# Residual rows and staged operand sums bound to fixed units of the products, and an earlier load of one pair of weights

## The chip, the cores and the metric

The kernel runs on one core of a Trainium2 chip. The time is what the device takes for one launch, in microseconds (us), as the median of several runs. The engines are named as in the profile: PE is TensorE, DVE is VectorE, ACT is ScalarE, POOL is GpSimd, SP is SyncE, which here only issues DMAs.

## The reference

One layer of a hybrid decoder for a prompt of 2048 tokens (with 16 meta tokens ahead of it) and 8 sample tokens; D_MODEL is 1024, D_FF 4096, everything float32.

```python
def _layer(h, s0, buf, chunked, lb, norm1_g, w_in, ..., w_out, norm2_g, w_up, w_down):
    hn = _rmsnorm(h, norm1_g)
    z = jnp.einsum('btd,dc->btc', hn, w_in)
    ...                                    # HGRN2 recurrence || conformer convolution
    h = h + jnp.concatenate([y_hg, y_cv], axis=-1) @ w_out
    hn2 = _rmsnorm(h, norm2_g)
    h = h + jnp.square(jax.nn.relu(hn2 @ w_up)) @ w_down
    return h, s_new, new_buf
...
    y_prompt = _rmsnorm(hp[:, N_META:], final_g)
    y_sample = _rmsnorm(hs, final_g)
```

The change touches the last part, the MLP (`w_up`, squared ReLU, `w_down`, residual, final norm), and the loads ahead of it.

## The kernel before

**Mixer.** About the first 990 us compute the input projection, the recurrence, the convolution and the out-projection, by quarters of the tokens (`q`) and tiles of output columns (`t`). The out-projection leaves h, transposed, in the DRAM tensor `hscr`, and the row of each token's norm factor in `mscr`. Each product is done in fp32r with every operand split in a rounded high half (`hi`) and the rest (`lo`).

**MLP.** The tokens go in three passes `p` (688, 688 and 680 columns; pass 0 holds 680 of the prompt and the 8 of the sample). D_FF goes in 16 groups `g` of 256. A *unit* is twelve matmuls. The up-projection of a group is a Strassen-Winograd scheme of seven products, in the order P1, P5, P6, P3, P7, P2, P4: seven U units, whose epilogues leave the squared ReLU in `hid`. The down-projection of a group is eight D units, whose epilogues add into `acc`. The list `seq` sets the order: in a pass seven U units of group 0; then seven U of group 1 and eight D of group 0; then, from group 2 on, a U unit of group g and a D unit of group g-1 in turn; at the end eight D units of the last group. `steps` holds the position in `seq` of each group's first U unit, over all passes.

**Operands.** `op` and `extra` hold the split token sums that the seven products take, the weight sums of w_up lie in `ups` and `wsp`, and the pieces of w_down come as `junk` or `wsp` (`d_load`, `d_split`). The sums of w_up for the next group, or pair, are made from loads into `raw`, `bst` or `acc` (`up_prep`); their loads and splits are put at units by a dictionary `hooks`, run right after the unit of that number. The operands of pass 0 are made on the fly (`h_first`, `h_rest`). Those of passes 1 and 2 are staged: `h_stage(p + 1)` computes 4 x 7 sums while pass p runs, each as ScalarE high half and VectorE low half in the one buffer `stg`, which SP then stores to `bop_d` in DRAM. In the last group of pass p, as each product gives its operands back, `h_fetch` loads those of the next pass from `bop_d`, 28 transfers in all.

**What sets the order.** Beside the units runs a planner: background tasks (`bg`) are generators which say before each step what engine it is for (`yield "act"`); a model of the engines' times (`model`) puts such steps, by the task's number, where it thinks the engine free. Three such tasks matter here. `residual(p)`, number 6, starts with the first U unit of pass p: it takes both tiles of `xns`, loads the norm row, and for each of 8 row blocks loads a row of `hscr` into the tile `xn`, multiplies it on POOL and adds it into `acc` on VectorE. `h_stage(p + 1)`, number 7, is added after U0 of group 2 and takes the same two tiles. In the last group the program says

```python
if g == NG - 1 and p < NPASS - 1:
    bg.until(lambda: ("staged", p + 1) in done)
    h_fetch(p + 1, PRODUCTS[d][3])
```

which runs the generators until all sums are issued. `fg_load` and `eps_cols` (the row of final_g, and 19 small loads of `emm` out of `mscr`) are added ahead of the first unit of the MLP. The finishing of a pass (`finish`) transposes finished tiles into two free PSUM banks.

**At the entry of the MLP** the weights of the second pair (`up_prep(1)`) go to a tile `raw` and three buffers that are taken from `scr` after the mixer; their four loads are hooks of the first U units.

## Time and profile before

| | us |
|---|---|
| median of 3 runs | 2554.85 |
| the runs | 2554.21, 2554.85, 2560.22 |
| the profiled execution, its own time | 2564.89 |
| its span | 2563.2 |
| PE busy | 2326.5 (91%) |
| DVE busy | 1684.5 (66%) |
| ACT busy | 1055.4 (41%) |
| POOL busy | 666.1 (26%) |

The profile is of one execution; all times that are read from its rows are in us from the start of its span. The mixer ends and the MLP begins at about 987, pass 1 begins at 1555, pass 2 at 2069. Every operation stands at line 146, a helper that records them all, so rows are told apart by their tiles.

### The profile page before, as it was taken

How to read it: one execution, taken by the hardware profiler on the slowest of the kernel's cores; microseconds unless marked ns; L12 is line 12 of the kernel's file. 1: busy time of each engine (PE TensorE's matmuls, PEld its weight loads, DVE VectorE, ACT ScalarE, POOL GpSimd, SP SyncE). 2: the span in 40 equal slices, each digit the busy share in tenths (PEclk: the TensorE clock that was granted, in tenths of full speed). 3: DMA queues.
4: the chain of work that ended last, by engine and by line, in shares of the span. 5: the costliest groups of instructions: out<-in, count | busy, mean ns of one | idle time of the engine just before them, and what ended most of it. 6: DMA issues, size and time to landing. Idle time of an engine off the chain costs nothing.

```text
span 2563.2 us, 37257 instructions
## 1 busy us (share of the span) xinstructions
PE 2326.5 (91%) x13790; PEld 2170.7 (85%) x13790; DVE 1684.5 (66%) x2906; ACT 1055.4 (41%) x2199; POOL 666.1 (26%) x529
## 2 busy tenths in 40 slices
PE   8888899899999996999999848999999689999998
PEld 8877678777877875899999837999999689999997
DVE  7797977488478545467666635577777555765665
ACT  6454544444354333444544424333333333333332
POOL 5552424333254012244333211111010011211000
PEclk9998899999999997999999969999999899999999
DMA  8665346834644474355455474445444634443332
GB/s 300 214 203 173 136 176 206 287 132 164 227 169 161 175 257 137 118 159 166 164 188 181 140 249 150 131 129 156 153 153 151 240 122 134 134 121 119 107 107 102
DMA packets 309470, 428.71 MB, mean 167 GB/s; under 512 B 21506, under 2 KB 216391, under 8 KB 292896
## 3 DMA queue, kind: packets, MB, share of 16 engines
q1 hardware_dynamic: 309144, 426.06, 50.8%
q8 instruction: 109, 1.79, 0.3%
q14 instruction: 73, 0.60, 0.1%
q10 hardware_dynamic: 144, 0.26, 0.0%
HBM read 311.75 MB, written 114.97 MB: 166 GB/s over the span
## 4 chain that ended last, share of the span: by engine, by line
PE 46%; DVE 20%; issue 11%; DMA 10%; ACT 5%; POOL 4%; SPq 2%; POOLq 0%; ACTq 0%; DVEq 0%
PE ps L146 46%; DVE ps L146 7%; DMA junk<-in_w_down_dram 4%; SPq L146 2%; DVE stat L146 2%; POOL wsp L146 2%; DMA bst<-in_w_up_dram 2%; DVE acc L146 2%; ACT cst L146 1%; DMA bop_d<-stg 1%; DVE cst L146 1%; POOL ups L146 1%; DVE I L146 1%; DVE kept L146 1%; DVE raw L146 1%
## 5 line engine op out<-in xcount | busy, mean ns | idle before, releaser
L146 PE MATMUL ps<-op,wsp 128*128 128x512 f32 (+6 forms) x5427 | 1063.5, 350 | 23.2 <-DVE op L146 12.4
L146 PEld LDWEIGHTS ps<-op,wsp 128*128 128x128 f32 x5427 | 893.5, 194 | 127.6 <-DVE op L146 14.1
L146 PE MATMUL ps<-hid,wsp 128*128 128x344 f32 (+2 forms) x4512 | 779.9, 324 | 95.3 <-DVE acc L146 61.9
L146 PEld LDWEIGHTS ps<-hid,wsp 128*128 128x128 f32 x4512 | 728.5, 191 | 110.3 <-ACT wsp L146 38.6
L146 DVE TENSOR_TENSOR acc<-ps,acc 128x688 f32<-128x688 f32 (+4 forms) x424 | 346.5, 818 | 319.4 <-PE ps L146 259.6
L146 ACT ACTIVATE cst<-cst 128x344 f32<-128x344 f32 (+1 forms) x384 | 188.4, 491 | 466.6 <-DVE cst L146 460.2
L146 PE MATMUL ps<-op,ups 128*128 128x344 f32 (+1 forms) x2013 | 354.6, 324 | 15.9 <-DVE cst L146 7.2
L146 PEld LDWEIGHTS ps<-op,ups 128*128 128x128 f32 x2013 | 327.7, 192 | 20.0 <-DVE cst L146 6.3
L146 POOL TENSOR_TENSOR acc<-acc 128x512 f32<-128x512 f32 x169 | 225.1, 1332 | 244.4 <-ACT acc L146 227.6
L146 DVE SCALAR_TENSOR_TENSOR ps<-glu,cw,ps 128x512 f32<-128x512 f32 x295 | 221.7, 751 | 5.9
L146 POOL TENSOR_TENSOR wsp<-junk,wsp 128x256 fp32r<-128x256 f32 x128 | 101.7, 796 | 371.2 <-ACT wsp L146 332.0
L146 DVE TENSOR_TENSOR cst<-ps,cst 128x344 f32<-128x344 f32 (+1 forms) x336 | 170.9, 509 | 19.2 <-PE ps L146 15.7
L146 POOL TENSOR_TENSOR ups<-bst,ups 128x512 fp32r<-128x512 f32 x50 | 76.6, 1541 | 297.8 <-ACT ups L146 297.8
L146 DVE TENSOR_TENSOR hid<-cst,hid 128x344 fp32r<-128x344 f32 (+1 forms) x192 | 105.5, 549 | 56.4 <-ACT hid L146 56.1
L146 DVE TENSOR_TENSOR ups<-raw,ups 128x512 fp32r<-128x512 f32 x108 | 79.9, 740 | 89.6 <-ACT ups L146 89.4
L146 POOL TENSOR_TENSOR wsp<-bst,wsp 128x512 fp32r<-128x512 f32 x42 | 63.5, 1521 | 251.3 <-ACT wsp L146 251.3
L146 ACT ACTIVATE acc<-glu,cw 128x512 f32<-128x512 f32 x185 | 123.5, 715 | 1.6 <-DVE glu L146 1.6
L146 DVE TENSOR_TENSOR wsp<-raw,wsp 128x512 fp32r<-128x512 f32 x84 | 64.2, 765 | 57.8 <-ACT wsp L146 57.5
L146 POOL TENSOR_TENSOR wsp<-raw,wsp 128x1024 fp32r<-128x1024 f32 (+1 forms) x34 | 79.1, 2327 | 76.5 <-ACT wsp L146 63.8
L146 ACT ACTIVATE wsp<-junk 128x256 fp32r<-128x256 f32 x128 | 52.2, 409 | 110.5 <-DMA junk<-in_w_down_dram 94.5
L146 ACT ACTIVATE hid<-cst 128x344 fp32r<-128x344 f32 (+1 forms) x192 | 94.2, 491 | 6.1
L146 ACT ACTIVATE wsp<-raw 128x512 fp32r<-128x512 f32 (+1 forms) x118 | 85.9, 728 | 10.8 <-DMA raw<-in_w_in_dram 6.6
(239 smaller groups left out, 2098.0 us busy)
## 6 DMA issues: line engine op xcount, KB each, us to landing
wsp<-kw SPq DMA_DIRECT2D x96, 1024.0 KB, 4.8
wsp<-down_w SPq DMA_DIRECT2D x248, 256.0 KB, 2.7
bst<-in_w_up_dram SPq DMA_DIRECT2D x138, 256.0 KB, 4.7
kw<-wsp SPq DMA_DIRECT2D x32, 1024.0 KB, 5.0
down_w<-wsp SPq DMA_DIRECT2D x128, 256.0 KB, 2.0
bop_d<-stg SPq DMA_DIRECT2D x56, 344.0 KB, 2.7
junk<-in_w_down_dram SPq DMA_DIRECT2D x128, 128.0 KB, 3.4
raw<-in_w_in_dram SPq DMA_DIRECT2D x24, 512.0 KB, 7.7
```

The source lines that it names most:

```text
L146: return fn(*args, **kw)
```

## The change

- **Residual rows and staged sums.** `residual` and `h_stage` are gone. `side_work(p)` returns a list of (unit, function), counted from U0 of group 2 of the pass, which goes into `hooks`. The row block k of the residual is loaded at unit 4k, multiplied at 4k + 2 and added at 4k + 3. From unit 33 on, four blocks of 31 units follow (passes 0 and 1): the two loads, and seven sums at 3, 7, 11, 15, 19, 23 and 28, ScalarE's half at that unit, VectorE's half and the store one unit later. The wait ahead of `h_fetch` has become an assertion.
- **Second pair's weights.** The task `up_first`, which prepares the first pair, takes the three buffers of `scr` as soon as the last input of the out-projection is loaded, and issues the four loads there; the hooks leave them out.
- **fg and emm.** These two tasks are added at the first unit of group 3 of pass 0.
- **Finishing.** `finish` tells the model when its two banks come free.

```diff
@@ -801,6 +801,11 @@
             if n_ == late[0]:
                 scr.give(*got)
+                yield from until(("last out",))
+                up_raws[1] = yield from take(scr, 3)
+                yield "sp"
+                for f in up_prep(1)[0:4]:
+                    f[3]()
                 yield from until(("mix",))
...
                     out_load(q, t)
+                    if q == NQ - 1 and t == K8 - 1:
+                        done.add(("last out",))
...
-        up_raws[1] = [b[:, 0:512] for b in scr.take(3)]
...
-        def residual(p):
...
-            for k in range(K8):
-                yield "sp"
-                h_load(t, p, k)
...
-                yield "pool"
-                G.tensor_tensor(t[:, 0:n], t[:, 0:n], msb[:, 0:n], ALU.mult)
-                yield "dve"
-                V.tensor_tensor(acc[:, k, 0:n], acc[:, k, 0:n], t[:, 0:n], ALU.add)
...
-        def h_stage(p):
...
-            def emit(i, idx, src, scale):
-                yield from split_sum(stg[:, 0, 0:n], stg[:, 1, 0:n], src, scale)
-                yield "sp"
-                SP.dma_start(bop_d[p - 1, i, idx], flat32(stg))
...
+        def side_work(p):
...
+            def rows(k):
+                def times():
...
+                    G.tensor_tensor(t[:, 0:n], t[:, 0:n], tt[:, 0:n], ALU.mult)
+
+                def add():
+                    V.tensor_tensor(acc[:, k, 0:n], acc[:, k, 0:n], t[:, 0:n], ALU.add)
+                    done.add(("res", p, k))
+
+                return [(4 * k, lambda: h_load(t, p, k)), (4 * k + 2, times), (4 * k + 3, add)]
+
             for k in range(K8):
...
+                work += rows(k)
+            at = 4 * K8 + 1
+
+            def staged(i, at):
...
+                def emit(at, idx, src, scale):
+                    def high():
+                        S.activation(hi, src, AF.Copy, scale=1.0 if scale is None else scale)
+
+                    def low():
...
+                        SP.dma_start(bop_d[p, i, idx], flat32(stg))
+
+                    return [(at, high), (at + 1, low)]
+
+                return ([(at, loads)] + emit(at + 3, B11, b11, g) + emit(at + 7, B21, b21, gg) +
+                        emit(at + 11, B22, b22, gg) +
+                        [(at + 14, scaled), (at + 14, lambda: V.tensor_tensor(t1, b12, b11, ALU.subtract))] +
+                        emit(at + 15, T1, t1, g) + [(at + 18, mult_add(t2, t1, ng, t2, ALU.add))] +
+                        emit(at + 19, T2, t2, None) + [(at + 22, mult_add(t1, b21, gg, t2, ALU.subtract))] +
+                        emit(at + 23, T4, t1, None) +
+                        [(at + 26, scaled), (at + 27, mult_add(t2, b12, ng, t2, ALU.add))] +
+                        emit(at + 28, T3, t2, None))
+
+            if p < NPASS - 1:
+                for i in range(4):
+                    work += staged(i, at)
+                    at += 31
...
-            banks.items.remove(b)
-            banks.items.remove(b + 1)
+            for x in (b, b + 1):
+                banks.items.remove(x)
+                model.cur.t = max(model.cur.t, banks.t.get(x, 0.0))
...
-                    if n_ < 4 and G_ % NG == 0 and G_:
+                    if n_ < 4 and G_ == 0:
+                        continue
+                    if n_ < 4 and G_ % NG == 0:
                         at = a - 2
...
-        bg.add(fg_load(), 3)
-        bg.add(eps_cols(), 4)
+        for p in range(NPASS):
+            a = steps[p * NG + 2]
+            for at, f in side_work(p):
+                hooks.setdefault(a + at, []).append(f)
+        hooks[steps[3]].append(lambda: (bg.add(fg_load(), 3), bg.add(eps_cols(), 4)))
...
-                bg.add(residual(p), 6)
...
-                if g == 2 and d == 0 and p < NPASS - 1:
-                    bg.add(h_stage(p + 1), 7)
                 if g == NG - 1 and p < NPASS - 1:
-                    bg.until(lambda: ("staged", p + 1) in done)
+                    assert ("staged", p + 1) in done
                     h_fetch(p + 1, PRODUCTS[d][3])
```

How the order of the instructions changes, at three places. On SP at the entry of the MLP, behind the last store of a norm row (`mscr<-fg`), where `junk` are pieces of w_down, `in_w_up_dram` is the source of the second pair's weights and `down_w<-wsp_87` stores split pieces of w_down; before:

```order
L146 DMA mscr<-fg 1x512
L146 DMA junk<-in_w_down_dram 128x2x128 x2
L146 DMA down_w<-wsp_87 128x512 x2
L146 DMA junk<-in_w_down_dram 128x2x128 x2
L146 DMA fg<-in_final_g_dram 128x1024
L146 DMA emm<-mscr 128x1 x5
```

And after:

```order
L146 DMA mscr<-fg 1x512
L146 DMA raw_85<-in_w_up_dram 128x4x128
L146 DMA acc<-in_w_up_dram 128x4x128 x3
L146 DMA junk<-in_w_down_dram 128x2x128 x2
L146 DMA down_w<-wsp_87 128x512 x2
```

The four loads of the second pair stood behind all of emm and now stand ahead of the first two junk pieces; fg and emm are gone from here, and stand, in the same order, in group 3 of pass 0, behind four loads of weights.

On SP at the end of pass 0, in the last group, where `bop_d<-stg` stores a staged sum, `xn` are the rows from which the sums are made, and `op<-bop_d` is the fetch for pass 1; before:

```order
L146 DMA junk<-in_w_down_dram 128x2x128
L146 DMA bop_d<-stg 128x688 x4
L146 DMA xn_90<-hscr 128x688
L146 DMA xn_91<-hscr 128x688
L146 DMA bop_d<-stg 128x688 x7
L146 DMA op_83<-bop_d 128x2x344 x2
L146 DMA op_84<-bop_d 128x2x344 x2
```

And after:

```order
L146 DMA down_w<-wsp_87 128x512
L146 DMA junk<-in_w_down_dram 128x2x128
L146 DMA op_83<-bop_d 128x2x344 x2
L146 DMA op_84<-bop_d 128x2x344 x2
L146 DMA raw_85<-in_w_up_dram 128x4x128
```

The last eleven stores and the loads for seven of them have left this place; they stand spread between the units of the earlier groups, and the same is so at the end of pass 1.

On DVE at the entry of the MLP, where `raw_85` and `raw_86` take sums of the second pair's weights (in `acc`) and the `op_84` rows are the low halves of pass 0's operands; before:

```order
L146 SCALAR_TENSOR_TENSOR op_84<-acc,vec,op_84 128x344
L146 TENSOR_TENSOR op_84<-bst_7385,op_84 128x344
L146 TENSOR_TENSOR op_84<-bst_7386,op_84 128x344
L146 TENSOR_TENSOR raw_86<-acc,raw_85 128x512
L146 TENSOR_TENSOR raw_85<-raw_85,acc 128x512
L146 TENSOR_TENSOR op_84<-bst_7385,op_84 128x344
L146 TENSOR_TENSOR op_84<-bst_7386,op_84 128x344
```

And after:

```order
L146 TENSOR_TENSOR op_84<-bst_7386,op_84 128x344
L146 TENSOR_TENSOR wsp_88<-raw_85,wsp_88 128x512
L146 SCALAR_TENSOR_TENSOR op_84<-xn_91,vec,op_84 128x344
L146 TENSOR_TENSOR wsp_88<-raw_86,wsp_88 128x512
L146 SCALAR_TENSOR_TENSOR op_84<-acc,vec,op_84 128x344
L146 TENSOR_TENSOR wsp_89<-raw_86,wsp_89 128x512
L146 TENSOR_TENSOR op_84<-bst_7385,op_84 128x344
L146 TENSOR_TENSOR op_84<-bst_7386,op_84 128x344
L146 SCALAR_TENSOR_TENSOR op_84<-xn_91,vec,op_84 128x344
L146 TENSOR_TENSOR raw_86<-acc,raw_85 128x512
L146 TENSOR_TENSOR raw_85<-raw_85,acc 128x512
```

Before, four low halves of this stretch stood ahead of the two sums that need the second pair's loads (`raw_86<-acc,raw_85` and `raw_85<-raw_85,acc`), and the rest of them behind; now the two sums stand behind more of the low halves and behind three splits of first-pair weights.

## Rows read from the trace of the kernel before

**Rows 1.** The page, part 1: engine, busy us (share of the span) x instructions.

```profile
PE 2326.5 (91%) x13790; PEld 2170.7 (85%) x13790; DVE 1684.5 (66%) x2906; ACT 1055.4 (41%) x2199; POOL 666.1 (26%) x529
```

**Rows 2.** The time line of TensorE around the end of pass 0. Columns: start us, duration us, engine, line, operation, output tile <- input tiles, shape, count; in brackets the idle time before it and what ended it. Rows of `op` with `wsp` or `ups` are U units, rows of `hid` are D units.

```profile
1458.29 2.04 PE L146 MATMUL ps<-op,wsp 128*128 128x344 f32 x12
...
1465.85 2.05 PE L146 MATMUL ps<-hid,wsp 128*128 128x344 f32 x12
1467.74 2.07 PE L146 MATMUL ps<-op,ups 128*128 128x344 f32 x12
1501.11 3.78 PE L146 MATMUL ps<-hid,wsp 128*128 128x344 f32 x12 [31.30 <-DVE acc L146]
...
1513.51 3.81 PE L146 MATMUL ps<-op,ups 128*128 128x344 f32 x12 [4.42 <-DVE cst L146]
...
1535.83 5.82 PE L146 MATMUL ps<-hid,wsp 128*128 128x344 f32 x24 [4.59 <-DVE acc L146]
1542.86 12.45 PE L146 MATMUL ps<-hid,wsp 128*128 128x344 f32 x72 [1.21 <-ACT wsp L146]
1555.14 3.46 PE L146 MATMUL ps<-op,wsp 128*128 128x344 f32 x21
```

**Rows 3.** The time line of SP's DMA queue, same place; the last row is the same at the end of pass 1. The duration of a merged row runs from the first issue to the end of the last.

```profile
1463.55 10.44 SPq L146 DMA_DIRECT2D bop_d<-stg  x4
...
1479.49 21.03 SPq L146 DMA_DIRECT2D bop_d<-stg  x7
1500.62 2.59 SPq L146 DMA_DIRECT2D op<-bop_d  x4
...
2015.85 2.51 SPq L146 DMA_DIRECT2D op<-bop_d  x4
```

**Rows 4.** Windows of 4 us, same place: stretch, its length, busy time (x instructions) of PE, PEld, DVE, ACT, POOL, then the granted TensorE clock, the mean share of the DMA engines, GB/s.

```profile
1516.00:1520.00 4.00, 4.00 (x17) 4.00 (x17) 2.88 (x6) 2.29 (x5) 0.50 (x1) 0.58 1.07 388
...
1540.00:1544.00 4.00, 2.79 (x17) 2.31 (x16) 1.40 (x2) 0.83 (x2) 0.87 (x2) 1.00 0.60 211
```

**Rows 5.** The time line of TensorE around the end of pass 1, columns as in rows 2.

```profile
1995.39 2.04 PE L146 MATMUL ps<-op,ups 128*128 128x344 f32 x12
...
2016.25 3.81 PE L146 MATMUL ps<-hid,wsp 128*128 128x344 f32 x12 [10.62 <-DVE acc L146]
...
2027.34 3.78 PE L146 MATMUL ps<-hid,wsp 128*128 128x344 f32 x12 [4.88 <-DVE raw L146]
...
2054.42 15.02 PE L146 MATMUL ps<-hid,wsp 128*128 128x344 f32 x84 [2.08 <-DMA wsp<-down_w]
2069.28 3.89 PE L146 MATMUL ps<-op,ups 128*128 128x340 f32 x24
```

**Rows 6.** The time line of TensorE at the entry of the MLP, columns as in rows 2.

```profile
987.47 2.09 PE L146 MATMUL ps<-op,ups 128*128 128x344 f32 x6
...
995.15 5.24 PE L146 MATMUL ps<-op,ups 128*128 128x344 f32 x17 [2.25 <-DVE op L146]
...
1011.24 1.23 PE L146 MATMUL ps<-op,wsp 128*128 128x344 f32 x3 [9.63 <-DVE op L146]
...
1034.65 3.59 PE L146 MATMUL ps<-op,wsp 128*128 128x344 f32 x12
...
1066.29 2.05 PE L146 MATMUL ps<-op,wsp 128*128 128x344 f32 x12
```

**Rows 7.** The time line of SP's DMA queue at the entry of the MLP.

```profile
988.28 0.24 SPq L146 DMA_DIRECT2D mscr<-fg  x1
988.57 0.90 SPq L146 DMA_DIRECT2D junk<-in_w_down_dram  x2
...
995.10 8.73 SPq L146 DMA_DIRECT2D emm<-mscr  x19
1003.93 0.38 SPq L146 DMA_DIRECT2D raw<-in_w_up_dram  x1
```

**Rows 8.** The time line of VectorE at the entry of the MLP.

```profile
1007.65 0.69 DVE L146 TENSOR_TENSOR raw<-acc,raw 128x512 f32<-128x512 f32 x1 [9.27 <-DMA acc<-in_w_up_dram]
```

**Rows 9.** The time line of ScalarE at the entry of the MLP.

```profile
990.70 0.42 ACT L146 ACTIVATE wsp<-junk 128x256 fp32r<-128x256 f32 x1 [1.85 <-DMA junk<-in_w_down_dram]
...
991.63 0.57 ACT L146 ACTIVATE op<-xn,vec 128x344 fp32r<-128x344 f32 x1
```

**Rows 10.** What is done with the tiles xn between 1060 and 2300 us: engine, operation, output <- input, count, duration in ns (smallest/median/largest), first and last start; below, who waited for these instructions (us, times), and the time from issue to landing of the loads.

```profile
L146 DVE SCALAR_TENSOR_TENSOR stg<-xn,vec,stg x32: 559/566/1175, 1203.6 to 2004.7; 128x344 fp32r<-128x344 f32 x16, 128x340 fp32r<-128x340 f32 x16
L146 POOL TENSOR_TENSOR xn<-xn,xn x24: 1632/1672/2127, 1092.5 to 2247.3; 128x688 f32<-128x688 f32 x16, 128x680 f32<-128x680 f32 x8
...
  DVE acc L146: 5.4, 3
...
DMA to landing us min/median/max: 3.6/4.2/5.8
```

**Rows 11.** The time line of TensorE at the start of pass 1, columns as in rows 2. `ident,acc` are the transposes of finished tiles.

```profile
1562.87 1.22 PE L146 MATMUL ps<-ident,acc 128*128 128x128 f32 x8 [2.05 <-DVE xn L146]
...
1569.17 1.09 PE L146 MATMUL ps<-ident,acc 128*128 128x128 f32 x8 [1.37 <-DVE xn L146]
...
1597.57 1.69 PE L146 MATMUL ps<-ident,acc 128*48 128x128 f32 x8 [2.62 <-DVE xn L146]
```

**Rows 12.** One window of 32 us in the middle of pass 1, columns as in rows 4.

```profile
1856.00:1888.00 32.00, 32.00 (x206) 32.00 (x205) 21.35 (x33) 10.99 (x22) 3.44 (x2) 1.00 0.52 167
```

More of the change, by code (lines that the diff above doesn't have):

```diff
@@ L1610, in eps_cols @@
             done.add(("emm",))
-        def residual(p):
-            yield from until(*[("st", q) for q in quarters(p)], *[("acc", p, k) for k in range(K8)])
-            t, msb = yield from take(xns, 2)
-            yield "sp"
-            SP.dma_start(msb[:, 0:PROMPT[p]],
-                         mscr[:, T0[p]:T0[p] + PROMPT[p]].to_broadcast([P, PROMPT[p]]))
-            if p == 0:
-                SP.dma_start(msb[:, PROMPT[p]:PN[p]], mscr[:, SEQ:SEQ + NS].to_broadcast([P, NS]))
-            n = PN[p]
-            for k in range(K8):
-                yield "sp"
-                h_load(t, p, k)
-                if p == 0:
-                    yield "act"
-                    S.activation(t[:, PROMPT[0]:PN[0]], hsT[:, k], AF.Copy)
-                yield "pool"
-                G.tensor_tensor(t[:, 0:n], t[:, 0:n], msb[:, 0:n], ALU.mult)
-                yield "dve"
-                V.tensor_tensor(acc[:, k, 0:n], acc[:, k, 0:n], t[:, 0:n], ALU.add)
-                done.add(("res", p, k))
-            xns.give(t, msb)
```

61 lines of the change are left out of this document (32 added, 29 removed).

## The prediction

> **What bounds the kernel now.** I read the page first: TensorE is busy 91% of the span [rows 1], so nothing off its path counts unless TensorE waits for it. Then I took the time line of TensorE and looked for the gaps, and for each gap the time line of the engine named in it. A unit of the MLP (twelve matmuls, one U or D) takes 1.89 us when nothing is missing: the units that start at 1465.85 and 1467.74 [rows 2]. Three places are far from that.
>
> *End of pass 0.* From 1458.29 (U0 of the last group) to 1555.14 (first unit of pass 1) are 96.9 us [rows 2] for 7 + 8 + 8 = 23 units, 43.5 us of work: 53.4 us too long. The largest piece is a gap of 31.30 us. In it SP only passes staged sums to DRAM, four and then seven in one row [rows 3]: the generator is run dry there, and each sum needs the one buffer stg, so ScalarE, VectorE and the DMA take turns, about 3 us a sum. VectorE has the accumulations of the units queued behind that chain, which is why the gap is put down to DVE acc. The granted clock stands at 0.58 after it [rows 4] (the 1.2 GHz level for part of the stretch), and two more waits follow, 4.42 and 4.59 us [rows 2]. In the last ones the DMA engines are full: share 1.07 at 388 GB/s, until it drops at 1540 [rows 4].
>
> *End of pass 1.* The same stretch, 1995.39 to 2069.28, is 73.9 us, 30.4 too long; its gaps are 10.62, 4.88 and, at the end of the full DMA, 2.08 us [rows 5].
>
> *Entry of the MLP.* From 987.47 to 1066.29 are 78.8 us for 22 units (41.6 us), 37.2 too long [rows 6]. The longest gap is 9.63 us on a VectorE operand split. VectorE was itself idle 9.27 us for a weight piece of the second pair [rows 8], since SP issued these loads at 1003.93, behind 19 small loads of emm that took 8.73 us [rows 7].
>
> **The change part by part.**
>
> *Staged sums at fixed units.* Nothing is computed that was not before; 56 sums and 24 residual rows move. In pass 0 and pass 1 the order shows no staged store left in front of the first operand fetch, so both gaps of the run-dry chain go. What is late next is the fetch itself: 28 transfers for the next pass, issued as each product releases its operands. They keep the DMA engines full from 1500.62 [rows 3] to about 1541 [rows 4], and TensorE's last wait in the stretch ends at 1542.86 [rows 2]. I therefore don't credit the gap but the shift of the fetch: it now starts when U0 is done, 1458.29 + 2.04 = 1460.3, instead of 1500.6. If the transfers then need as long as before, everything behind them comes 40.3 us earlier, and 13 us of the stretch's excess remain. Pass 1 likewise: the fetch starts after U0 (1995.39 + 2.04 = 1997.4 [rows 5]) in place of 2015.85 [rows 3], so 18 us. Bounds: if TensorE at full clock asks faster and loses to the full queue, the gain is less by the waits that follow the gap, 4.42 + 4.59 in pass 0 and 4.88 + 2.08 in pass 1, giving 31 and 11; if the queue is emptier than before since no staged store overlaps and the weights arrive in time, half of the same waits is gained, giving 44 and 22. I take **-40** and **-18**.
>
> *Second pair's weights and the emm loads.* The order puts the four loads behind the last mscr row, issued at 988.28, so not truly inside the out-projection but about 15 us earlier than 1003.93 [rows 7]. The 9.63 us gap goes. What takes its place: the two junk pieces now stand behind 1 MB of weights. ScalarE has their splits ahead of the operand splits of P1, and got the first at 990.70, about 2 us after issue, the operand split following at 991.63 [rows 9]. One of the four loads waits besides for GpSimd, which reads its buffer. The nearest row for four such loads is 1003.93 to 1007.65, when VectorE gets its first [rows 7, 8]; so junk lands near 995.5, not 990.7. TensorE took up P1 at 995.15 [rows 6] because of VectorE, so of these 5 us about 2 reach it (bounds 0 and 5). Behind the gap, from 1011.24 to 1034.65, TensorE spent 23.4 us on some 53 matmuls, worth 8.3 at 1.89 us for twelve: 15.1 us in small waits and low clock while VectorE caught up [rows 6]. Without the 9 us of standing still it has less to catch up, but the same splits, sums and epilogues stay in its queue; I take half back, 7.5, bounds 0 and 12. Sum -9.6 + 2 - 7.5 = **-15**, bounds -5 and -22.
>
> The pages have a word on the 5 us. The Trainium skill (DMA: Bandwidth & Descriptors, Queues, rings and completion order) says that each DMA engine consumes descriptors of one ring in ring order, which speaks against putting 1 MB ahead of the junk pieces: by it ScalarE stands to about 995.5. Were the pieces served side by side, 993 would do and this part would be worth -17 instead of -15. The row of 990.70, with nothing ahead, doesn't decide between them.
>
> The fg and emm loads now go out in group 3 of pass 0 and hold SP for 8.73 us and a bit there [rows 7]. Queued behind: stores of split down weights and junk loads. A junk piece is asked for four units (7.6 us) ahead of its split and split again four units ahead of its use, so a delay of 8 us holds ScalarE for some 4 us and should just miss TensorE: +1, bounds 0 and 6.
>
> *Residual rows at fixed units.* Each row is load at unit 4k, product on GpSimd at 4k + 2, add on VectorE at 4k + 3; the add stands in VectorE's queue, so if the product is late, every epilogue behind it is too. A load lands in 3.6 to 5.8 us, the product takes 1.67 [rows 10]: 5.3 to 7.5 against the 5.7 us between the points. Before, VectorE waited for products 5.4 us in all [rows 10]. VectorE is busy about 21 of 32 us here [rows 12], and a bank is written again three units after its epilogue fell due, which lets it be behind by some 3 us, so an overrun of 1 us is mostly swallowed. 28 sums now share the groups of pass 0, where 17 did before the eleven of the gap [rows 3]; at 0.57 us for the low half [rows 10] and four more such instructions for seven sums that is some 10 us more VectorE work spread over 245 us. I take +2 for all passes; the bounds are -4 (a few of the small waits at group ends go) and +12 (half a us for each of 24 rows).
>
> *Finishing tiles.* The planner now books a bank's release time, so the transposes move away from the places where TensorE waited 2.05 and 1.37 us for a bank [rows 11]. In exchange the fifth tile now stands directly before the sixth, where 2.62 us were waited already, and both ahead of the first D unit. Gain and loss about cancel: -1, bounds -6 and +5.
>
> *Sum.* -40 - 18 - 15 + 1 + 2 - 1 = -71. The profiled execution took 2564.89 us, so one like it would take 2493.9. It lies 10.0 above the median of the runs, 2554.85; I assume that this distance stays as it is, so the forecast is 2554.85 - 71 = **2484 us**. All good bounds together give -98 (2457), all bad ones -24 (2531); neither is likely as a whole.
>
> **Rivals.**
>
> *The fetch takes it back.* At full clock the products release operands faster than the DMA engines serve, TensorE stalls again inside the group and loses its clock again. For it: share 1.07 already [rows 4]. Against: the fetch was paced by the same units before. With 25 and 5 us gained at the two pass ends the sum is -43: 2512.
>
> *Entry unchanged.* The junk wait on ScalarE and VectorE's own work replace the 9.63 us. For it: 15.1 us of excess that have no single cause [rows 6]. The sum is -56: 2499.
>
> *Entry free.* The entry goes at TensorE's pace after P1 and keeps the clock, and the weights come in time at the pass ends: some -95, 2460.
>
> *Slower: adds that stand.* Place: the residual add in VectorE's queue, 24 times. If a landing plus product overran the 5.7 us by more than the 3 us of slack plus 3.0 us each, 24 x 3.0 = 72 us would eat the whole gain; at 3.4 us the time is 2484 + 82 = 2566. That needs landings of 10 us and more, where the rows show at most 5.8 [rows 10].
>
> *It doesn't do it.* Staged work still waiting at the fetch would leave 2540 to 2555. The order has no staged store there, so this is nearly excluded.
>
> **How the numbers follow.** Forecast (2465 to 2508) 0.60; the fetch takes it back 0.13; entry unchanged (its time lies within the forecast's spread, told apart by the profile only) 0.12; entry free 0.09; slower 0.03; doesn't do it 0.03. The range 2460 to 2520 takes in the first four but for their tails. About 0.3% (7.7 us) is what a measurement of this kernel can tell from no change: faster by more 0.94, within 0.03, slower 0.03.
>
> **What would show it.** Right: no TensorE gap over 12 us in the last groups of passes 0 and 1; the stretch from U0 of the last group to the next pass near 56 us in both; DMA share near 1 right after U0; second-pair loads issued near 989; ScalarE waiting for junk until about 995; the entry near 64 us for its 22 units. Wrong: long waits of VectorE for GpSimd in groups 2 and 3 of each pass; a group 3 of pass 0 that is several us longer than its neighbours; stretches at the pass ends of 65 us and more.

## The result and the profile after

The changed kernel takes 2528.47 us (median of 4 runs, 2525.32 to 2529.94) against 2557.53 us for the kernel before in the same comparison: a ratio of 0.9884, 95% interval 0.9863 to 0.9904. The forecast was 2484 us, with 2460 to 2520 as its range: the sign was right, the size was not. The profiled execution took 2529.94 us, 35.0 less than the one of before (2564.89), and it is this difference that the stages below split up. It lies 1.5 us above the median of its kernel, where the profiled execution of before lay 10.0 above; the prediction had taken that distance for constant, and so the medians moved by 29.1 only.

The stages, worked out from TensorE's time line by counting matmuls (twelve a unit; a stage ends where the named unit starts; us; differences are of unrounded times). "Entry" is the 22 units of groups 0 and 1, "last" runs from U0 of the last group to the next pass. The expectations below go by a count that comes out up to 1 us shorter in the longer stages:

```
                   start  entry  p0 g2-4  p0 g5-14  p0 last  p1 entry  p1 g2-14  p1 last  p2 entry  p2 rest   span
before             987.5   78.8     92.8     299.2     96.9      62.0     378.2     73.9      60.8    433.1  2563.2
after              987.8   67.5    120.0     311.6     57.2      57.9     384.9     53.5      57.3    430.6  2528.2
difference          +0.3  -11.3    +27.2     +12.4    -39.6      -4.2      +6.7    -20.4      -3.5     -2.5   -35.0
forecast                    -15   { +3, of it 2 for all passes }  -40               -18                         -71
```

Both pass ends did what was forecast. TensorE's time line of the changed kernel at the end of pass 0, to be read against [rows 2]:

```profile
1486.84 2.04 PE L146 MATMUL ps<-op,wsp 128*128 128x344 f32 x12
...
1517.66 3.50 PE L146 MATMUL ps<-hid,wsp 128*128 128x344 f32 x12 [2.47 <-ACT wsp L146]
1524.58 5.34 PE L146 MATMUL ps<-hid,wsp 128*128 128x344 f32 x24 [3.42 <-DVE acc L146]
1531.64 12.61 PE L146 MATMUL ps<-hid,wsp 128*128 128x344 f32 x72 [1.72 <-ACT wsp L146]
1544.08 1.57 PE L146 MATMUL ps<-op,wsp 128*128 128x344 f32 x9
```

And at the end of pass 1, against [rows 5]:

```profile
1986.88 2.05 PE L146 MATMUL ps<-op,ups 128*128 128x344 f32 x12
...
2016.60 2.13 PE L146 MATMUL ps<-hid,wsp 128*128 128x344 f32 x12 [2.27 <-DMA wsp<-down_w]
2020.91 2.52 PE L146 MATMUL ps<-hid,wsp 128*128 128x344 f32 x12 [2.19 <-DMA wsp<-down_w]
2025.17 15.32 PE L146 MATMUL ps<-hid,wsp 128*128 128x344 f32 x84 [1.74 <-DMA wsp<-down_w]
2040.34 1.56 PE L146 MATMUL ps<-op,ups 128*128 128x340 f32 x9
```

The gaps of 31.30 and 10.62 us are gone. What is late next is a split, an epilogue and, in pass 1, the loads of split weights, 7.6 and 6.2 us of waits. The fetch now starts just after U0 in both passes, as SP's time line of the changed kernel has it:

```profile
1489.65 2.57 SPq L146 DMA_DIRECT2D op<-bop_d  x4
...
1987.54 2.50 SPq L146 DMA_DIRECT2D op<-bop_d  x4
```

From the start of the fetch to the end of TensorE's last wait are 42.0 us in pass 0 (1489.65 to 1531.64) and 42.2 before (1500.62 to 1542.86 [rows 2, 3]); in pass 1 37.6 (1987.54 to 2025.17) and 38.6 before (2015.85 to 2054.42 [rows 3, 5]). So the end of the stretch moved with the fetch.

The DMA share stands at 1.06 soon after, with TensorE at full clock; a window of 4 us of the same kernel, columns as in rows 4:

```profile
1500.00:1504.00 4.00, 4.00 (x28) 4.00 (x27) 3.05 (x7) 1.08 (x4) 0.54 (x1) 1.00 1.06 368
```

The loss sits in the middle of pass 0: U0 of the last group stood at 1458.29 before and stands at 1486.84 now, 28.6 us later, though the entry had brought 11. Groups 2, 3 and 4 take 39.1, 44.6 and 36.2 us, where they took 30.0, 33.5 and 29.3. The time line of TensorE of the changed kernel in groups 2 to 4 shows it:

```profile
1072.20 2.69 PE L146 MATMUL ps<-hid,wsp 128*128 128x344 f32 x12 [3.53 <-DVE acc L146]
...
1091.09 3.44 PE L146 MATMUL ps<-hid,wsp 128*128 128x344 f32 x12 [3.88 <-DVE acc L146]
...
1119.60 3.81 PE L146 MATMUL ps<-op,ups 128*128 128x344 f32 x12 [9.07 <-DVE cst L146]
...
1145.90 3.78 PE L146 MATMUL ps<-hid,wsp 128*128 128x344 f32 x12 [4.84 <-DVE acc L146]
```

Each of these releasers is an epilogue on VectorE. What VectorE itself waited for stands in its waits from 1060 to 1160 us (waiting engine and tile, releaser, us in total, times, longest); the changed kernel:

```profile
DVE acc L146 <- POOL xn L146: 34.3, 6, 12.5
```

The kernel before, same stretch:

```profile
DVE acc L146 <- POOL xn L146: 1.8, 2, 1.6
```

So the adds of the residual rows stand for GpSimd's product. How the longest of the six comes about is read across four engines. SP of the changed kernel:

```profile
1100.50 10.07 SPq L146 DMA_DIRECT2D emm<-mscr  x19
1110.67 0.38 SPq L146 DMA_DIRECT2D down_w<-wsp  x1
1111.09 0.43 SPq L146 DMA_DIRECT2D junk<-in_w_down_dram  x1
1111.62 0.45 SPq L146 DMA_DIRECT2D xn<-hscr  x1
```

ScalarE, GpSimd and VectorE (three time lines of the same kernel):

```profile
1114.46 0.42 ACT L146 ACTIVATE wsp<-junk 128x256 fp32r<-128x256 f32 x1 [11.84 <-DMA junk<-in_w_down_dram]
```

```profile
1116.07 1.63 POOL L146 TENSOR_TENSOR xn<-xn,xn 128x688 f32<-128x688 f32 x1 [14.42 <-DMA junk<-in_w_down_dram]
```

```profile
1069.89 1.38 DVE L146 TENSOR_TENSOR acc<-acc,xn 128x688 f32<-128x688 f32 x1 [9.72 <-POOL xn L146]
...
1117.74 1.38 DVE L146 TENSOR_TENSOR acc<-acc,xn 128x688 f32<-128x688 f32 x1 [12.52 <-POOL xn L146]
1119.04 1.06 DVE L146 TENSOR_TENSOR cst<-ps,cst 128x344 f32<-128x344 f32 x2
```

The 19 emm loads hold SP for 10.07 us; behind them stand the junk piece and the row; the product starts 4.45 us after the row is issued, the add after that, and only then the epilogue `cst` that TensorE waits for (9.07 us).

The first of the six needs no emm: its row is issued at 1062.23, behind the four weight loads of the group and the norm row, and its add, due at unit 3, starts at 1069.89 after 9.72 us of standing. While GpSimd stands for that product, a weight split whose ScalarE half was done at 1062.07 stands behind it; the store of the split holds SP, and the next row stands behind the store. So one late row makes the next one late (GpSimd, then SP, of the changed kernel; the profile puts the product's wait down to a store issued just after the row):

```profile
1068.21 1.64 POOL L146 TENSOR_TENSOR xn<-xn,xn 128x688 f32<-128x688 f32 x1 [9.16 <-DMA down_w<-wsp]
1069.82 2.04 POOL L146 TENSOR_TENSOR wsp<-junk,wsp 128x256 fp32r<-128x256 f32 x2
```

```profile
1062.23 0.43 SPq L146 DMA_DIRECT2D xn<-hscr  x1
...
1070.56 0.32 SPq L146 DMA_DIRECT2D down_w<-wsp  x1
...
1071.47 0.43 SPq L146 DMA_DIRECT2D xn<-hscr  x1
```

SP stood for GpSimd's splits before the change too. Its waits from 1060 to 1160 us, in the kernel before:

```profile
SPq L146 <- POOL wsp L146: 59.0, 23, 7.2
```

And in the changed kernel:

```profile
SPq L146 <- POOL wsp L146: 57.0, 14, 8.4
```

At the entry the 9.63 us gap is gone and another has come; TensorE's time line, against [rows 6]:

```profile
987.77 1.76 PE L146 MATMUL ps<-op,ups 128*128 128x344 f32 x6
997.20 0.65 PE L146 MATMUL ps<-op,ups 128*128 128x344 f32 x1 [7.66 <-ACT op L146]
998.25 4.56 PE L146 MATMUL ps<-op,ups 128*128 128x344 f32 x17 [0.40 <-DVE op L146]
...
1010.84 3.81 PE L146 MATMUL ps<-op,wsp 128*128 128x344 f32 x12 [4.25 <-DVE cst L146]
...
1021.82 3.21 PE L146 MATMUL ps<-extra,ups 128*128 128x344 f32 x9 [4.39 <-ACT extra L146]
```

ScalarE had its first junk split at 990.70 before [rows 9]; now:

```profile
995.90 0.77 ACT L146 ACTIVATE wsp<-junk 128x256 fp32r<-128x256 f32 x2 [6.80 <-DMA junk<-in_w_down_dram]
```

The four weight loads, issued from 989.18, delay the first use of the junk pieces to about the 995.5 that the prediction worked out. TensorE's wait for ScalarE's half of P1 before the change, ahead of the row of 995.15 [rows 6], was

```profile
992.25 0.66 PE L146 MATMUL ps<-op,ups 128*128 128x344 f32 x1 [2.70 <-ACT op L146]
```

It waits 5 us longer for that half now, but 1.85 us less for VectorE's half behind it (0.40 against 2.25). The 17 matmuls that follow start 10.5 us after the first matmul of the MLP, where they started 7.7 us after it: of the 5.2 us of delay, 2.8 reached TensorE.

### The profile page after: what moved, and what is told of

Its sections match the earlier page's. It is cut to its first block, busy times and chain, and to the rows that moved or that the text cites. A ratio compares the mean times of both kernels' runs of the same rounds, so it can differ in the third digit from the quotient of the medians.

```text
span 2528.2 us, 37232 instructions
## 1 busy us (share of the span) xinstructions
PE 2323.0 (92%) x13790; PEld 2169.1 (86%) x13790; DVE 1689.7 (67%) x2906; ACT 1054.9 (42%) x2199; POOL 662.2 (26%) x529
## 4 chain that ended last, share of the span: by engine, by line
PE 48%; DVE 22%; issue 10%; DMA 9%; ACT 6%; POOL 3%; SPq 2%; POOLq 0%; ACTq 0%; DVEq 0%
PE ps L146 48%; DVE ps L146 6%; DVE acc L146 2%; DVE stat L146 2%; ACT cst L146 2%; DMA junk<-in_w_down_dram 2%; SPq L146 2%; DVE cst L146 2%; POOL wsp L146 1%; DVE raw L146 1%; DMA acc<-xscr 1%; DVE I L146 1%; DMA raw<-in_w_in_dram 1%; DVE kept L146 1%; ACT wsp L146 1%
## 5 line engine op out<-in xcount | busy, mean ns | idle before, releaser
L146 PEld LDWEIGHTS ps<-hid,wsp 128*128 128x128 f32 x4512 | 729.2, 191 | 86.9 <-issue 29.1
```

Source lines behind the costliest of these rows:

```text
L146: return fn(*args, **kw)
```

## The experiments

Three theories for the loss in pass 0. A: the adds stand in VectorE's queue because their rows come late. B: the emm batch alone. C: VectorE is full in pass 0, wherever things stand. Every kernel here was timed against the kernel before; the ratio stands with its interval. The median of the kernel before lay between 2557.5 and 2566.5 us in these comparisons, so a difference of medians from two of them is good to some us only. Times of stages are of one execution each: five kernels with the staged sums of pass 0 at the same units differ by 4 us in groups 5 to 14 (310.9 to 314.9).

**emm_spread.** One emm load every third unit from group 5 on.

```diff
-        hooks[steps[3]].append(lambda: (bg.add(fg_load(), 3), bg.add(eps_cols(), 4)))
+        hooks[steps[5]].append(lambda: bg.add(fg_load(), 3))
+        for i, f in enumerate(eps_parts()):
+            hooks.setdefault(steps[5] + 3 * i, []).append(f)
```

> The changed kernel, but the 19 emm loads (and fg) no longer go out in one batch in group 3 of pass 0: from group 5 on, one emm load every third unit. Theory A (the residual adds stand in VectorE's queue because their rows come late, for want of room on SP's queue): only the part of group 3 goes in which SP was held by the batch, 9.07 us of TensorE's gap, so groups 2 to 4 of pass 0 take about 110 us instead of 120 and the whole is 8 to 11 us shorter. Theory B (the batch alone makes the loss): groups 2 to 4 fall to about 95, the whole is 20 to 25 us shorter. Theory C (VectorE is full in pass 0, whatever stands where): no change beyond 3 us.

2513.78 us, 0.981 (0.9782 to 0.9837). Groups 2 to 4 take 110.9 us instead of 120.0: 9.1 us, the length of the gap. A's number, not B's; part of the total's further fall lies in a mixer 2.9 us shorter in this execution, in groups 5 to 14 (1.6) and in pass 1.

**rows0_six.** Six units for a row of pass 0, emm batch left in place.

```diff
-                return [(4 * k, lambda: h_load(t, p, k)), (4 * k + 2, times), (4 * k + 3, add)]
+                w, m, d = (6, 4, 5) if p == 0 else (4, 2, 3)
+                return [(w * k, lambda: h_load(t, p, k)), (w * k + m, times), (w * k + d, add)]
...
-            at = 4 * K8 + 1
+            at = (6 if p == 0 else 4) * K8 + 1
```

> The changed kernel, but in pass 0 a residual row takes six units instead of four: load at 6k, product at 6k + 4, add at 6k + 5, staged sums 16 units later; the emm batch stays in group 3. Theory A: the add is due 3.8 us later behind its load, so most waits of VectorE for the product of 2 to 5 us go and the long one at the batch stays or shrinks: groups 2 to 4 about 105 us instead of 120, the whole 10 to 15 us shorter. Theory B: within 4 us of the changed kernel. Theory C: no change beyond 3 us.

2514.58 us, 0.9812 (0.9779 to 0.9845). Groups 2 to 4 take 109.5 us, 10.5 less with the batch still in place: B falls, and A's 105 is not reached; C falls too, since the same adds cost less where they stand wider. VectorE's waits for the product from 1050 to 1150 fall from 29.7 us in the changed kernel to

```profile
DVE acc L146 <- POOL xn L146: 8.3, 4, 2.8
```

**rows0_eight_emm.** Both, with (8, 5, 7) for a row; the staged sums of pass 0 begin 32 units later.

```diff
+                w, m, d = (8, 5, 7) if p == 0 else (4, 2, 3)
...
+            for i, f in enumerate(eps_parts()):
```

> The changed kernel with the emm loads spread as in the other run and in pass 0 eight units for a residual row: load at 8k, product at 8k + 5, add at 8k + 7. Theory A: VectorE no longer waits for products, groups 2 to 4 of pass 0 take 90 to 95 us (92.9 before the change), the whole is 22 to 28 us shorter than the changed kernel. Theory B: no better than the emm run by itself. Theory C: no change beyond 3 us, or the loss moves to groups 5 to 14, which gain what groups 2 to 4 lose.

2501.70 us, 0.9768 (0.974 to 0.9796). Groups 2 to 4 take 94.8 us, so the wider rows are worth another 16.1 beside the spread emm loads; with them two staged sums left group 4, for which the price of no_sums0 below gives about 1 us. VectorE's waits for the product, same stretch:

```profile
DVE acc L146 <- POOL xn L146: 3.7, 2, 1.8
```

**rows0_planner_emm.** The task `residual(0)` brought back for pass 0 with emm spread.

```diff
+                    bg.add(residual(0), 6)
...
-            at = 4 * K8 + 1
+            at = 4 * K8 + 1 if p else 74
...
-                    at += 31
+                    at += 31 if p else 30
```

> The changed kernel with the emm loads spread and the residual rows of pass 0 put by the planner as before the change (a task of number 6 from the first unit of the pass); the staged sums stay at fixed units, from unit 74 on, 30 units for four rows' seven sums. Theory A: groups 2 to 4 about 93 us as before the change, the whole 22 to 28 us shorter than the changed kernel. If the staged sums at fixed units cost something by themselves, groups 7 to 14 stay some 10 us above those of before.

2505.07 us, 0.978 (0.9747 to 0.9813). Groups 2 to 4 take 92.0 us, before the change 92.8. A holds: the rows' fixed places and the emm batch together, with the two sums of group 4, are the whole loss of these groups. But groups 5 to 14 take 319.7 us with the 28 sums pressed into eight groups: the sums cost something by themselves.

**junk_first.** From rows0_eight_emm: the four weight loads out of `up_first` and behind the first `d_load(1)`.

```diff
                     d_load(1)
+                    bg.until(lambda: 1 in up_raws)
+                    for f in up_prep(1)[0:4]:
+                        f[3]()
                     d_split(1)
```

> From the kernel with spread emm loads and eight units for a residual row of pass 0 (2501.7 us, entry of the MLP 68.1 us): the first two junk pieces go out ahead of the second pair's four loads, which follow at once. Theory J (the pieces behind 1 MB of weights hold ScalarE and so TensorE at the entry, 7.66 us in the profile of the changed kernel where 4.95 were waited before): that wait falls back to about 5 us and the entry to 63 to 66 us, the whole by 2 to 5. Theory V (VectorE's own work sets the entry): the wait moves to the next place, entry within 1 us of 68.

2497.32 us, 0.9742 (0.9725 to 0.9759). TensorE's first wait falls from 8.82 to 2.76 us, the one behind it rises from 0.38 to 2.16, and the 17 matmuls of P1 start 7.7 us after the first matmul of the MLP instead of 11.1. The entry falls from 68.1 to 64.4, as theory J has it.

**weights_late.** The same loads put behind `bg.wait(done, ("ups",))`, after the second two junk pieces.

```diff
                     bg.wait(done, ("ups",))
+                    for f in up_prep(1)[0:4]:
+                        f[3]()
```

> From the same kernel: the early issue of the second pair's weights undone, the four loads follow the first junk pieces, the stores of their splits and the next two pieces, as they did before the change, but without fg and emm ahead of them. If the early issue is what took 11 us from the entry, it goes back to 75 to 79 us and the whole is 7 to 11 us longer. If moving emm away was what did it, the entry stays within 2 us of 68 or falls below it, since the junk pieces are free again.

2494.71 us, 0.9736 (0.9715 to 0.9757). The entry takes 58.5 us, 9.6 less. TensorE's time line:

```profile
986.39 0.66 PE L146 MATMUL ps<-op,ups 128*128 128x344 f32 x1 [3.62 <-ACT op L146]
989.21 4.46 PE L146 MATMUL ps<-op,ups 128*128 128x344 f32 x17 [2.16 <-DVE op L146]
...
1001.34 3.81 PE L146 MATMUL ps<-op,wsp 128*128 128x344 f32 x12 [3.89 <-DVE cst L146]
```

The 17 matmuls of P1 start 7.7 us after the first matmul of the MLP, as in junk_first; so the loads' place ahead of the junk pieces cost about 3.4 us. The other 5.9 us against junk_first come behind P1: here the planner also puts the sums of these weights behind more of the operands' low halves on VectorE. That order wasn't tried by itself.

**before_emm.** The kernel before, with fg and the emm loads as in emm_spread, and nothing else.

```diff
-        bg.add(fg_load(), 3)
-        bg.add(eps_cols(), 4)
+        hooks[steps[5]].append(lambda: bg.add(fg_load(), 3))
+        for i, f in enumerate(eps_parts()):
+            hooks.setdefault(steps[5] + 3 * i, []).append(f)
```

> The kernel before, with one thing alone: the 19 emm loads and fg no longer go out at the entry of the MLP but from group 5 of pass 0 on, one emm load every third unit. If the entry's loss was the emm batch ahead of the second pair's weights, and not the place of those weights in the code, the entry falls from 78.8 us to 57 to 62 and the whole by 17 to 22 us. If the early issue is needed, the entry stays above 70.

2551.14 us, 0.9954 (0.9939 to 0.997). The entry falls from 78.8 to 68.2 us, between the two expectations: moving emm away is worth 10.7 us, nearly all that the change gained there (11.3). The other 9.7 us down to 58.5 don't come from SP: SP issues the four loads 7.6 us after the first matmul of the MLP in both kernels (993.12 after 985.51 here, 989.18 after 981.56 in weights_late), and P1's 17 matmuls start 7.7 us after it in both. What differs behind that is the order on ScalarE and VectorE, where the sums of these weights stand ahead of low halves here and behind them in weights_late.

**finish_undone.** From rows0_eight_emm: the two lines in `finish` as before.

```diff
-            for x in (b, b + 1):
-                banks.items.remove(x)
-                model.cur.t = max(model.cur.t, banks.t.get(x, 0.0))
+            banks.items.remove(b)
+            banks.items.remove(b + 1)
```

> From the same kernel: the planner no longer books the time at which a finishing tile's banks come free. If that booking took the 4.6 and 3.6 us from the entries of passes 1 and 2 (62.1 and 61.1 before the change, 57.6 and 57.0 now), they return and the whole is 6 to 9 us longer. If they come from the residual rows, which start in group 2 now and not at the first unit, the entries stay within 1 us and so does the whole. As the prediction had it (gain and loss cancel): 1 us longer.

2511.96 us, 0.9802 (0.9783 to 0.9821), 10.3 us longer by the medians of two comparisons. The entries of passes 1 and 2 rise by only 1.4 and 0.6 us (59.2, 57.9), the rest of pass 2 by 6.4 (436.9). The waits of [rows 11] in kind are back at the very end, where the two sets of tiles meet the last D units; TensorE's time line of this kernel:

```profile
2485.73 1.09 PE L146 MATMUL ps<-ident,acc 128*128 128x128 f32 x8 [1.52 <-DVE xn L146]
...
2489.71 1.05 PE L146 MATMUL ps<-ident,acc 128*40 128x128 f32 x8 [1.51 <-DVE xn L146]
```

**no_sums0.** From rows0_eight_emm: no instructions on ScalarE and VectorE for 27 sums of pass 0.

```diff
                     def high():
+                        if p == 0 and (i, idx) != (0, B11):
+                            return
...
                     def low():
+                        if p == 0 and (i, idx) != (0, B11):
+                            SP.dma_start(bop_d[p, i, idx], flat32(stg))
+                            return
```

> From the same kernel: leaves out ScalarE's and VectorE's work for 27 of the 28 staged sums of pass 0 (the loads and stores stay, so passes 1 and 2 get wrong operands). Groups 5 to 14 of pass 0 take 311 us with the sums, 298 before the change with 17 of them there, 283.5 would be their work alone. If the sums' instructions in VectorE's and ScalarE's queues make the difference, they fall to 290 to 298 us and the whole is 13 to 20 us shorter. If the stores and loads on SP do, they stay above 306.

2487.11 us, 0.9702 (0.9682 to 0.9722). Groups 5 to 14 take 296.7 us instead of 311.9: 15.2 us for 27 sums, 0.56 us each. The instructions cost, not the transfers; the stores stay, but no longer wait for VectorE's half. Where the planner places the sums they cost less: groups 9 to 12 take 118.5 us here with no sum, 118.2 in the kernel before with nine, 118.3 in before_emm with seven, and 123.9 to 131.5 in the kernels with twelve or more sums at fixed units.

**all_eight.** From weights_late: (8, 5, 7) in all passes.

```diff
-                w, m, d = (8, 5, 7) if p == 0 else (4, 2, 3)
+                w, m, d = (8, 5, 7) if True else (4, 2, 3)
...
-            at = (8 if p == 0 else 4) * K8 + 1
+            at = 8 * K8 + 1
```

> The kernel with spread emm loads, eight units for a residual row of pass 0 and the second pair's weights behind the junk pieces (2494.7 us), now with eight units in passes 1 and 2 as well. If adds that stand cost something there too (groups 2 to 14 of pass 1: 384 us in the changed kernel, 377 before the change), pass 1 gains 3 to 5 us in these groups and pass 2 some 2 us: the whole 4 to 8 us shorter. If the sums make that difference, nothing beyond 2 us.

2481.81 us, 0.9678 (0.9659 to 0.9698), the fastest of all. Groups 2 to 14 of pass 1 take 375.4 us instead of 381.1, the rest of pass 2 425.6 instead of 430.6. VectorE's waits for the product in groups 2 to 6 go from 4.8 and 6.2 us to none: the adds stood there too.

**sums_35.** From all_eight: six units a row, 35 units for seven sums.

```diff
-                w, m, d = (8, 5, 7) if True else (4, 2, 3)
+                w, m, d = (6, 4, 5) if True else (4, 2, 3)
...
-                    at += 31
+                    at += 35
```

> As the kernel with eight units in all passes, but six units for a residual row and 35 units, not 31, for a block of seven staged sums (a sum every five units, not four). In groups 5 to 14 of pass 0 ScalarE waited 16.7 us for the store of the sum before to release the one buffer stg. If that wait delays the weight splits behind it and so TensorE, the groups 5 to 14 fall from 314 us to 300 to 307 us; groups 2 to 4 rise by some 4 to 6 us with the narrower rows; the whole is 3 to 8 us shorter. If the sums' instructions cost by their mere time in VectorE's queue, groups 5 to 14 fall by no more than 3 us and the whole is some 3 to 5 us longer.

2504.64 us, 0.9768 (0.9752 to 0.9785): longer, and not for the reason that either theory gave. ScalarE's waits for the store of the sum before, from 1140 to 1440 us, are gone:

```profile
ACT stg L146 <- DMA bop_d<-stg: 2.0, 3, 0.7
```

where all_eight has

```profile
ACT stg L146 <- DMA bop_d<-stg: 15.6, 8, 5.2
```

Yet groups 5 to 14 take 322.4 us, 8.9 more, and groups 2 to 4 102.1, 5.6 more with the narrower rows. The theory of the one buffer falls. With 35 units a block and 15 a group, nearly all sums fall on the same three places of a group or one unit ahead of them; from the start of a group's first unit to that of its second are 4.2 us on average here, 3.6 in all_eight, 3.0 without sums (a unit alone is 1.89).

**pool_store.** From all_eight: the sums stored from GpSimd's queue.

```diff
-                        SP.dma_start(bop_d[p, i, idx], flat32(stg))
+                        G.dma_start(bop_d[p, i, idx], flat32(stg))
```

> As the kernel with eight units in all passes, but the staged sums are stored from GpSimd's queue instead of SP's, where they stand behind stores of weight splits. If SP's queue is what holds stg, ScalarE's waits for the stores fall from 16.7 us to under 8 and groups 5 to 14 from 314 us to 302 to 309. If not, or if GpSimd's splits now stand behind the stores, they stay or rise by up to 10 us.

2487.71 us, 0.9704 (0.9683 to 0.9725). Groups 5 to 14 take 320.0 us, and ScalarE's waits for the store stay (18.3 us). But the stores stand in GpSimd's queue now, and GpSimd stands there for VectorE's halves (1140 to 1440 us):

```profile
POOL bop_d L146 <- DVE stg L146: 42.4, 19, 7.7
```

So another queue doesn't end the waits; whether SP's queue lengthened them isn't told apart.

**phased** and **phased_off.** From all_eight: the sums locked to the groups, and the same nine units earlier (66 in place of 75). By that edit ScalarE's halves of phased_off stand at units 8, 11 and 14 of one group, 2, 9 and 12 of the next and 0 of the third; its expectation names other places. In phased_off the rows for the first sums are loaded over the last residual row between its product and its add, so that one block of the residual is replaced.

```diff
-            at = 8 * K8 + 1
+            at = 75
...
+                return (emit(at + 2, B11, b11, g) + emit(at + 5, B21, b21, gg) + emit(at + 8, B22, b22, gg) +
...
-                    at += 31
+                    at += 30
```

> As the kernel with eight units for a row in all passes (2481.8 us; groups 5 to 14 of pass 0 312.7 us), but the staged sums are locked to the groups: 30 units for seven sums, ScalarE's halves at units 2, 5, 8 and 11 of one group and 3, 6 and 9 of the next. Theory P (a sum costs when it falls on the boundary of a group, where ScalarE is full and VectorE stands behind it): groups 5 to 14 fall to 297 to 304 us, the second unit of a group back to 3.1 us, the whole 8 to 15 us shorter. Theory Q (a sum costs its time in VectorE's queue wherever it stands): groups 5 to 14 stay at 308 us or more.

> The same kernel with all sums nine units earlier, so that ScalarE's halves stand at units 11 and 14 of one group, 2, 5 and 12 of the next and 0 and 3 of the third. Theory P: groups 5 to 14 take 312 to 322 us, as many as with the uneven distances or more, and the kernel is 8 to 20 us slower than the phased one. Theory Q: the two are within 3 us of each other.

2483.84 us, 0.9701 (0.968 to 0.9721), and 2500.93 us, 0.9767 (0.9741 to 0.9793). The two are 17 us apart, 10.9 of them in groups 5 to 14 (317.7 and 328.5). But in groups 9 to 12, where each holds fourteen sums, they take 131.5 and 131.3 us: there the nine units make no difference. The rest lies in groups 5 to 8 (124.0 and 131.7), where phased_off's first sums and loads meet the last residual rows, and in the last two. So this pair doesn't decide between P and Q. P falls as it stood, since its places are no better in pass 0 than the uneven ones (317.7 against 313.5 in all_eight). Against Q speaks that five kernels with the uneven places take 123.9 to 129.3 us for the same fourteen sums, less than phased; this is a matter of 2 to 8 us in single executions, so it is not settled.

In phased the second group of each pair takes 32 to 36 us, the first 28 to 31. The loads of the next rows stand in unit 11 of the second group, but they aren't needed for it: the last second group has none and takes 33.1, and group 6 has two and no sum and takes 29.0.

In pass 1 the same places do better: groups 2 to 14 take 371.5 us in phased, 375.4 in all_eight and 375.6 in phased_off, and their units alone would be 368.6. In pass 1 the weights come split from DRAM; what of this makes the difference wasn't tried.

## Why the prediction was wrong, step by step

**Staged sums out of the pass ends: right.** -40 and -18 forecast, -39.6 and -20.4 measured, by the mechanism that was given: credit the shift of the fetch, not the gap. The time from the fetch to the end of the last wait stayed as it was (42.0 and 42.2 us in pass 0).

**The step that failed: "Residual rows at fixed units", +2 us with bounds -4 and +12, and with it the fg and emm loads, +1 us with bounds 0 and 6.** Together groups 2 to 14 of pass 0 lost 39.6 us and those of pass 1 lost 6.7. The prediction compared landing plus product, 5.3 to 7.5 us, with the 5.7 us between load and add [rows 10], as if a load were issued at its unit and the product ran when it landed. In pass 0 neither holds: SP stands before stores that wait for weight splits, and GpSimd before splits that wait for junk, so the chain starts late and VectorE stands for it, 34.3 us in six waits in 100 us. The landing itself is as the rows had it: the first five products start 4.4 to 6.0 us after their row is issued.

For the load on the engines the prediction looked at VectorE alone, in a window of pass 1 [rows 12], where GpSimd is busy 3.44 of 32 us. In groups 2 to 4 of pass 0 of the kernel before (window, columns as in rows 4) VectorE is as busy, but GpSimd is busy 37.41 of 92.60 us, mostly with weight splits:

```profile
1066.30:1158.90 92.60, 87.70 (x540) 86.37 (x540) 60.00 (x86) 38.25 (x87) 37.41 (x34) 0.98 0.52 163
```

That window, and SP's 59.0 us of standing there, could have been read beforehand.

The runs split the loss in groups 2 to 4, 27.2 us, in the order in which they undo it: 9.1 for the emm batch (emm_spread), 16.1 for four units a row with the two sums of group 4 (rows0_eight_emm), 2.0 for the rest. In another order the shares differ: six units a row bring 10.5 with the batch in place. The same mechanism was in the prediction as the rival "adds that stand", dismissed for want of landings of 10 us; the lateness was not in the landing but ahead of the issue. Two of the prediction's own signs of being wrong came: VectorE's long waits for GpSimd in groups 2 and 3, and a group 3 of pass 0 that is 5.5 and 8.4 us longer than its neighbours (3.5 and 4.2 before the change).

**Also mis-sized in that step: the extra sums.** The prediction put the extra VectorE work of eleven more sums at some 10 us and called it spread and so covered. Groups 5 to 14 lost 12.4 us, and 27 sums left out give 15.2 back. So it wasn't the eleven alone that cost: at fixed units nearly all sums did, where the planner's cost little (no_sums0). VectorE was busy 205.8 of 300 us there before the change (1140 to 1440 us), but not evenly: TensorE loses 1.1 us on average ahead of the second unit of a group even without sums, and 1.5 to 2.3 with them at fixed units. What place would be free in pass 0 stays open: the wait for the one buffer is excluded as the cause (sums_35), SP's queue and the place in the group are not settled.

**Second pair's weights: size nearly right, the early issue not needed for it.** -15 forecast, -11.3 measured. The prediction's cause of the gap, loads late behind emm, holds: before_emm shows 10.7 us for moving emm alone. The early issue costs some 3.4 us in P1 (rows0_eight_emm against junk_first and weights_late). The Trainium skill (DMA: Bandwidth & Descriptors, Queues, rings and completion order) has a DMA engine consume one ring in order. The row of 995.90 agrees: it is nearer to 995.5 than to the 993 of pieces served side by side. The prediction let 2 of the 5 us reach TensorE, and 2.8 did. Behind P1 the entry gained 14.1 us (71.1 before, from 995.15 to 1066.29; 57.0 now, from 998.25 to 1055.26), where 9.6 and 7.5 were forecast. The 9.7 us that weights_late gains over before_emm come with the order on ScalarE and VectorE; what in that order makes them is open.

**Finishing tiles: -1 forecast, some 8 us measured.** The change took 10.2 us from the entries of passes 1 and 2 and from the rest of pass 2; undoing the booking gives 8.4 back in these three stages, 6.4 of it in the rest of pass 2, which the prediction didn't look at. The entries' gain is largely of another origin (1.4 and 0.6 of it return), the residual rows' start in group 2 being the candidate that wasn't tried by itself.

**The sum** of what was measured: 0.3 - 11.3 + 39.6 - 39.6 + 6.7 - 20.4 - 10.2 = -34.9 of the 35.0 us. With emm spread, the rows eight units wide and the weights behind the junk pieces the kernel takes 2481.81 us. That this is about the 2484 of the forecast is a coincidence: other terms make it up.

## What to carry to other kernels

An instruction put at a fixed place in an in-order queue is a promise that its whole chain is done by then: follow the chain back through every queue that it passes, to the point where its first transfer is issued, not where the code asks for it. Look at that chain in the stage where it will run, on every engine that it passes, and not in a calmer stage. Look for batches of small transfers in a queue that feeds a dense stage: 19 of them cost 9 to 11 us at both places where they stood in one piece, and nothing that could be seen when they went out one at a time. And after moving a large load earlier, look at what small piece now stands behind it.

## What the runs showed of the hardware

Nineteen loads of at most 128 values each held SP for 10.07 us in the middle of a dense stage, 0.53 us each, and for 8.73 us at the entry [rows 7]. Four loads of 256 KB ahead of two pieces of 128 KB in one queue delayed the pieces' first use by 5.2 us (990.70 to 995.90): they were issued 2.7 us later (988.57 and 991.26) and used 4.6 us after the issue instead of 2.1.
